# A hand-written schedule for every engine, half-batch broadcast tiles and later row sums in a three-point interpolation kernel

## The chip, the cores and the metric

The kernel runs on one core of a Trainium2 chip. The metric is the time of one execution in device microseconds. The engines are named as in the profile: PE multiplies matrices, PEld loads its weights, DVE works on vectors, ACT computes activations and copies, SP here only issues DMAs. The core has 16 DMA engines. A name with a q (SPq, ACTq) is an engine's sequencer issuing a DMA.

Only one core runs, so there is no other die to compare with. "Slow" here means only that a run was over 1.5% above the fastest run of the same kernel.

## The reference

For each of 16 batches, 4096 queries pick three of 1024 feature rows of 64 numbers and add them with normalized weights:

```python
batch, n_query, n_ref, dim = 16, 4096, 1024, 64
weights_norm = weights / (np.sum(weights, axis=2, keepdims=True) + 1e-8)
for b in range(batch):
    for i in range(n_query):
        for k in range(3):
            result[b, i] += weights_norm[b, i, k] * features[b, indices[b, i, k]]
```

## The kernel before

The gather is done as matrix products. A `prep` step on DVE turns indices into 16-bit codes and weights into two fp16 versions (for even and for odd rows), and writes both to DRAM. `load` broadcasts a batch's codes to all 128 partitions of SBUF, the on-chip memory (`bcc`), its even-row weights to partitions 0 to 63 and its odd-row weights to 64 to 127 (`bcw`), and loads and scales the features (`fst`, `f16`). Then, per group of 2048 queries, ACT makes `y` from the codes (`stage1`) and DVE makes four one-hot planes `s` (`stage2`). Per chunk of 512 queries PE multiplies features by `s` into `acc` (`main`), the result is weighted into `x` (on odd chunks through an ACT copy `xc`), and 12 small matmuls sum rows into `pr` (`back`), which ACT copies to `og` for the store.

```python
def load(b):
    bcc = sb.tile([P, K, Q], i16, bufs=2, name="bcc")
    nc.sync.dma_start(out=bcc[:, :, :], in_=code_d.ap()[b].unsqueeze(0).to_broadcast([P, K, Q]))
    bcw = sb.tile([P, K, Q], fp16, bufs=2, name="bcw")
    for h in range(2):
        nc.sync.dma_start(out=bcw[h * D:(h + 1) * D, :, :],
                          in_=wt_d.ap()[h, b].unsqueeze(0).to_broadcast([D, K, Q]))
    fst = sb.tile([P, J * P], fp32, bufs=2, name="fst")
    nc.scalar.dma_start(out=fst[:, :], in_=features[b].rearrange("(l x) d -> l (x d)", l=P))
    f16 = sb.tile([P, J, P], fp16, bufs=2, name="f16")
    nc.scalar.mul(out=f16.rearrange("p j m -> p (j m)"), in_=fst[:, :], mul=0.5)
    return bcc, bcw, f16
# ... cut: stage1, stage2, main, back ...
for i in range(NGT * NC):                  # 128 chunks
    g, c = divmod(i, NC)
    # ... cut: every 8 chunks prep of 4 batches and load(b + 1) ...
    if g + 1 < NGT:
        stage2(g + 1, c)
    x = main(i)
    if xs is not None:
        back(i - 1, xs)                    # row sums one chunk late
    xs = x
    if g + 2 < NGT and c > 0:
        stage1(g + 2, c - 1)
```

The program gives only this order; a scheduler decides where each instruction ends up on its engine.

Of the kernel before, what the change touches and what calls it, by code (L numbers as in the profile page):

```python
# [13 lines left out]
def kernel(  # L14
# [26 lines left out]
    GR = 2048  # L41
    NC = GR // CH
    NG = Q // GR
# [3 lines left out]
    Alu = mybir.AluOpType  # L47

# [6 lines left out]
    nc.sync.dma_start(out=i2[:, :], in_=i2_d.ap())  # L55
    bias_d = nc.inline_tensor((-8.0 * ((np.arange(P, dtype=np.float32) + 64) % 128 - 64))[:, None].copy(), name="lane")
    bias = sb.tile([P, 1], fp32, bufs=1, name="lane_sb")
    nc.sync.dma_start(out=bias[:, :], in_=bias_d.ap())
# [4 lines left out]
    def prep(b0):  # L63
        bs = slice(b0, b0 + PB)
        idx = sb.tile([P, PB, T, K], i64, bufs=1, name="idx")
        nc.sync.dma_start(out=idx[:, :, :, :],
                          in_=indices[bs].rearrange("b (p t) k -> p b t k", t=T))
        wt = sb.tile([P, PB, T, K], fp32, bufs=1, name="wt")
        nc.scalar.dma_start(out=wt[:, :, :, :],
                            in_=weights[bs].rearrange("b (p t) k -> p b t k", t=T))  # L70
        low = idx.bitcast(i32).rearrange("p b t (k w) -> p b k t w", k=K)[:, :, :, :, 0]
        idk = sb.tile([P, PB * K, T], i32, bufs=1, name="idk")
        nc.vector.tensor_copy(out=idk.rearrange("p (b k) t -> p b k t", b=PB), in_=low)  # L73
        lane = sb.tile([P, PB * K, T], i32, bufs=1, name="lane_i")
        nc.vector.tensor_scalar(out=lane[:, :, :], in0=idk[:, :, :], scalar1=6, scalar2=127 << 9,  # L75
                                op0=Alu.logical_shift_left, op1=Alu.bitwise_and)
        ex = sb.tile([P, PB * K, T], i32, bufs=1, name="ex")
        nc.vector.tensor_scalar(out=ex[:, :, :], in0=idk[:, :, :], scalar1=23, scalar2=3 << 24,
                                op0=Alu.logical_shift_left, op1=Alu.bitwise_and)
        ex2 = sb.tile([P, PB * K, T], i32, bufs=1, name="ex2")  # L80
        nc.vector.tensor_scalar(out=ex2[:, :, :], in0=ex[:, :, :], scalar1=134 << 23, scalar2=None,
                                op0=Alu.bitwise_xor)
        code = sb.tile([P, PB, K, T], u16, bufs=1, name="code")
        nc.vector.scalar_tensor_tensor(  # L84
            out=code.rearrange("p b k t -> p (b k t)"),
            in0=ex2.rearrange("p x t -> p (x t)").bitcast(fp32), scalar=0.5,
            in1=lane.rearrange("p x t -> p (x t)"), op0=Alu.mult, op1=Alu.add)
        hb = sb.tile([P, PB * K, T], i32, bufs=1, name="hb")
        nc.vector.tensor_scalar(out=hb[:, :, :], in0=idk[:, :, :], scalar1=1, scalar2=None,  # L89
                                op0=Alu.bitwise_and)  # L90
        ws = sb.tile([P, PB, T], fp32, bufs=1, name="ws")
        nc.vector.tensor_reduce(out=ws[:, :, :], in_=wt[:, :, :, :],  # L92
                                axis=mybir.AxisListType.X, op=Alu.add)
        nc.vector.tensor_scalar(out=ws[:, :, :], in0=ws[:, :, :], scalar1=1e-8, scalar2=None,
                                op0=Alu.add)
        wi = sb.tile([P, PB, T], fp32, bufs=1, name="wi")
        nc.vector.reciprocal(out=wi[:, :, :], in_=ws[:, :, :])  # L97
        wn = sb.tile([P, PB, K, T], fp16, bufs=1, name="wn")
# [32 lines left out]
    def stage1(g, k):  # L131
        b, gg = divmod(g, NG)
        if k == 0:
            ys[g] = sb.tile([P, K, GR], u8, bufs=2, name="y")
# [112 lines left out]
```

## Time and profile before

| | before |
|---|---|
| time, median (lowest to highest) | 523.24 us (522.9 to 523.54, 4 runs) |
| span of the profiled run | 521.9 us |
| first matmul | 63.0 us |
| DMA busy, all queues (85.5% of the span) | 446 us |
| ACT waiting for features | 2.3 us |

The page of the kernel before: span, PE's busy time, tenths busy in 40 slices of 13 us, and the main DMA queue (packets, MB, share of the 16 engines' span).

```profile
span 521.9 us, 7246 instructions
...
PE 402.1 (77%) x3072; PEld 203.2 (39%) x3072; DVE 303.9 (58%) x312; ACT 316.3 (61%) x242; POOL 0.2 (0%) x4
...
PE   0000188898988986898989797868989798989995
...
DMA  7999820798898879999999399999999899998421
...
q1 hardware_dynamic: 43296, 120.22, 81.9%
```

PE has nothing to do for 63 us and is then mostly 70 to 90% busy. The DMA engines, but for a gap in the start, are nearly always busy.

The windows view of the kernel before: busy time of each engine in each stretch, then the granted PE clock, the DMA share and GB/s. The first stretch loads `bcw`, the second `bcc`; the third is one cycle of a batch.

```profile
250.00:252.00 2.00, 2.00 (x22) 1.10 (x20) 0.00 (x0) 1.28 (x1) 0.00 (x0) 1.00 0.97 197
266.00:268.00 2.00, 2.00 (x21) 1.15 (x20) 1.29 (x2) 1.19 (x2) 0.00 (x0) 1.00 0.94 406
245.40:271.70 26.30, 24.49 (x193) 12.49 (x192) 16.61 (x16) 19.48 (x16) 0.00 (x0) 1.00 1.01 297
```

Both loads keep the engines busy, but `bcw` moves half as many bytes a second.

### The profile page before, as it was taken

The numbers are of one execution on the slowest core, as the hardware profiler recorded it, in microseconds if no ns is written. First come the engines' busy times: TensorE is split into PE (matmuls) and PEld (weight loads), VectorE is DVE, ScalarE is ACT, GpSimd is POOL, SyncE is SP. The second block draws the span as 40 slices with busy tenths as digits, with TensorE's granted clock in tenths as the row PEclk, the third lists the DMA queues.
The fourth block names the chain that finished last, engine by engine and source line by source line (L and its number), as shares of the span: only waits on it lengthen the run. The fifth ranks groups of instructions, "written<-read, shape, count | busy, mean of one in ns | idle before, by whom it ended". The sixth has DMA issues, their size and how long they took to land.

```text
span 521.9 us, 7246 instructions
## 1 busy us (share of the span) xinstructions
PE 402.1 (77%) x3072; PEld 203.2 (39%) x3072; DVE 303.9 (58%) x312; ACT 316.3 (61%) x242; POOL 0.2 (0%) x4
## 2 busy tenths in 40 slices
PE   0000188898988986898989797868989798989995
PEld 0000044444544443444544353434545354534443
DVE  5401375738584764656585855646585838484752
ACT  1006318667676838595868639385867768676733
POOL 0000000000000000000000000000000000000000
PEclk9999999998999999999999998989999999999998
DMA  7999820798898879999999399999999899998421
GB/s 187 339 195 315 167 51 30 299 218 329 202 343 213 172 284 224 377 215 374 215 377 215 112 315 211 370 212 374 212 372 212 325 230 332 235 331 203 124 80 42
DMA packets 47745, 125.67 MB, mean 241 GB/s; under 512 B 23136, under 2 KB 41568, under 8 KB 43616
## 3 DMA queue, kind: packets, MB, share of 16 engines
q1 hardware_dynamic: 43296, 120.22, 81.9%
q10 hardware_dynamic: 4416, 4.98, 3.2%
q8 instruction: 24, 0.39, 0.3%
q14 instruction: 9, 0.07, 0.1%
HBM read 107.23 MB, written 17.96 MB: 240 GB/s over the span
## 4 chain that ended last, share of the span: by engine, by line
PE 43%; ACT 19%; DMA 18%; issue 9%; DVE 9%; SPq 2%; DVEq 0%; ACTq 0%
PE acc L155 36%; ACT y L135 12%; DMA bcc<-code_d 8%; DMA wt<-in_weights_dram 8%; PE pr L177 7%; ACT xc L163 6%; DMA idx<-in_indices_dram 3%; DVE s L141 3%; DVE x L166 2%; DVE x L164 2%; SPq L111 1%; ACT og L184 1%; SPq L186 0%; SPq L120 0%; DVE idk L73 0%
## 5 line engine op out<-in xcount | busy, mean ns | idle before, releaser
L155 PE MATMUL acc<-s,f 128*128 128x512 fp8e4 x1536 | 367.3, 386 | 104.3 <-DVE s L141 70.5
L155 PEld LDWEIGHTS <-f 128*128 128x128 f16 x1536 | 143.7, 99 | 268.0 <-issue 114.9
L135 ACT ACTIVATE y<-bcc,lane_sb 128x2048 uint8<-128x2048 int16 x96 | 186.0, 1999 | 5.5 <-DMA bcc<-code_d 5.5
L141 DVE TENSOR_SCALAR s<-y 128x1536 int32<-128x1536 int32 x128 | 115.8, 955 | 64.2 <-ACT y L135 62.4
L163 ACT CAST xc<-acc 128x1536 f16<-128x1536 f32 x64 | 92.1, 1438 | 95.1 <-PE acc L155 95.1
L166 DVE TENSOR_TENSOR x<-acc,bcw 128x1536 f16<-128x1536 f32 x64 | 112.4, 1756 | 34.0 <-PE acc L155 33.5
L164 DVE TENSOR_TENSOR x<-xc,bcw 128x1536 f16<-128x1536 f16 x64 | 61.1, 955 | 69.7 <-ACT xc L163 69.7
L177 PEld LDWEIGHTS <-x 128*128 128x128 f16 x1536 | 70.0, 117 | 46.8 <-DVE x L164 18.6
L177 PE MATMUL pr<-i_sb,x 128*128 128x64 f16 x1536 | 72.8, 198 | 11.8 <-DVE x L164 10.0
L184 ACT COPY og<-pr 128x512 f32<-128x512 f32 x64 | 36.1, 588 | 60.7 <-PE pr L177 59.6
L92 DVE TENSOR_REDUCE ws<-wt 128x128 f32<-128x384 f32 x4 | 2.2, 550 | 41.8 <-DMA wt<-in_weights_dram 41.8
L135 ACT ACT_TABLE_LOAD x1 | 1.3, 1283 | 36.6 <-DVE wn L100 36.6
L125 ACT ACTIVATE f<-fst 128x512 f16<-128x512 f32 x16 | 10.1, 634 | 2.3 <-DMA fst<-in_features_dram 2.3
L73 DVE COPY idk<-idx 128x384 int32<-128x384 int32 x4 | 2.0, 504 | 3.4 <-DMA idx<-in_indices_dram 3.4
L97 DVE RECIPROCAL wi<-ws 128x128 f32<-128x128 f32 x4 | 3.8, 953 | 0.1
L100 DVE TENSOR_TENSOR wn<-wt,wi 128x128 f16<-128x128 f32 x12 | 3.3, 321 | 0.1
L125 ACT ACT_TABLE_LOAD x1 | 1.3, 1283 | 2.2 <-issue 2.2
L105 DVE TENSOR_TENSOR wh<-wn,hb 128x384 f16<-128x384 f16 x4 | 2.2, 556 | 0.0
L84 DVE SCALAR_TENSOR_TENSOR code<-ex,lane_i 128x384 uint16<-128x384 f32 x4 | 2.2, 554 | 0.0
L106 DVE TENSOR_TENSOR wh<-wn,wh 128x384 f16<-128x384 f16 x4 | 1.4, 359 | 0.1
L75 DVE TENSOR_SCALAR lane_i<-idk 128x384 int32<-128x384 int32 x4 | 1.4, 356 | 0.0
L89 DVE TENSOR_SCALAR hb<-idk 128x384 int32<-128x384 int32 x4 | 1.4, 358 | 0.0
(7 smaller groups left out, 4.2 us busy)
## 6 DMA issues: line engine op xcount, KB each, us to landing
bcc<-code_d SPq DMA_DIRECT2D x16, 3072.0 KB, 14.4
bcw<-wt_d SPq DMA_DIRECT2D x32, 1536.0 KB, 17.1
out_dram<-og SPq DMA_DIRECT2D x64, 256.0 KB, 7.4
fst<-in_features_dram ACTq DMA_DIRECT2D x16, 256.0 KB, 6.6
idx<-in_indices_dram SPq DMA_DIRECT2D x4, 384.0 KB, 5.0
wt<-in_weights_dram ACTq DMA_DIRECT2D x4, 192.0 KB, 10.2
wt_d<-wh SPq DMA_DIRECT2D x8, 96.0 KB, 7.0
code_d<-code SPq DMA_DIRECT2D x4, 96.0 KB, 7.3
```

What stands on the lines that cost most here:

```text
L97: nc.vector.reciprocal(out=wi[:, :, :], in_=ws[:, :, :])
L100: nc.vector.tensor_tensor(out=wn[:, :, k, :], in0=wt[:, :, :, k], in1=wi[:, :, :], op=Alu.mult)
L111: nc.sync.dma_start(out=wt_d.ap()[h, bs].rearrange("b k (p t) -> p b k t", t=T), in_=wh[:, h])
L125: nc.scalar.mul(out=f16.rearrange("p j m -> p (j m)"), in_=fst[:, :], mul=0.5)
L135: nc.scalar.activation(out=ys[g][:, k, :], in_=loaded[b][0][:, k, gg * GR:(gg + 1) * GR], func=Act.Abs_reciprocal_sqrt, bias=bias[:, :], s ...
L141: nc.vector.tensor_scalar(out=ss[g][:, j].rearrange("p k q -> p (k q)").bitcast(i32), in0=ys[g].rearrange("p k q -> p (k q)").bitcast(i32) ...
L155: nc.tensor.matmul(out=acc[:, k, :], lhsT=f16[:, j, :], rhs=s[:, j, k, c * CH:(c + 1) * CH], start=(j == 0), stop=(j == J - 1))
L163: nc.scalar.copy(out=xc[:, :, :], in_=acc[:, :, :])
L164: nc.vector.tensor_tensor(out=x[:, :, :], in0=xc[:, :, :], in1=w, op=Alu.mult)
L166: nc.vector.tensor_tensor(out=x[:, :, :], in0=acc[:, :, :], in1=w, op=Alu.mult)
L177: nc.tensor.matmul(out=pr[0][:, half, u, :], lhsT=x[:, k, :].rearrange("p (i u) -> p u i", u=U)[:, u, :], rhs=i2[:, :], start=(half == 0 a ...
L184: nc.scalar.copy(out=og[:, :, :, :], in_=pr[0][:, :, :, :])
```

## The change

The intent: no engine should idle because of the order a scheduler chose. Every instruction is kept in program order on its engine, and the program order is written out as a list of (time in chunks, step). The first batch is prepared alone and in small pieces, so that PE starts early. Broadcast tiles hold half a batch, with three buffers, and are asked for 12 chunks (codes) and 7 chunks (weights) ahead. All DMAs go through SP. The row sums of a chunk come two chunks late.

```diff
+    class InOrder:
+        def __getattr__(self, op):
+            def run(*a, **kw):
+                return tc.keep_in_program_order(getattr(self.engine, op)(*a, **kw))
+            return run
+    pe, ve, ac, sp = (InOrder(e) for e in (nc.tensor, nc.vector, nc.scalar, nc.sync))
 # ... cut ...
+    def load_codes(g):
+        b, q, n, _ = groups[g]
+        bcc[g] = sb.tile([P, K * GM], i16, bufs=3, name="bcc")[:, 0:K * n]
+        sp.dma_start(
+            out=bcc[g].rearrange("p (k q) -> p k q", k=K),
+            in_=code_d.ap()[b, :, q:q + n].unsqueeze(0).to_broadcast([P, K, n]))
 # ... cut: load_weights, the same with two halves of 64 partitions ...
+    def load_features(b):
         fst = sb.tile([P, J * P], fp32, bufs=2, name="fst")
-        nc.scalar.dma_start(out=fst[:, :], in_=features[b].rearrange("(l x) d -> l (x d)", l=P))
-        f16 = sb.tile([P, J, P], fp16, bufs=2, name="f16")
-        nc.scalar.mul(out=f16.rearrange("p j m -> p (j m)"), in_=fst[:, :], mul=0.5)
+        sp.dma_start(out=fst[:, :], in_=features[b].rearrange("(l x) d -> l (x d)", l=P))
+        f16s[b] = sb.tile([P, J, P], fp16, bufs=2, name="f16")
+        ac.mul(out=f16s[b].rearrange("p j m -> p (j m)"), in_=fst[:, :], mul=0.5)
 # ... cut ...
+    for g, (b, q, n, a) in enumerate(groups):      # a: first chunk of the group
+        m = n // CH
+        at(a - 12, 0, load_codes, g)
+        at(a - 7, 0, load_weights, g)
+        if q == 0:
+            at(a - 11.5 if b == 0 else a - 6, 0, load_features, b)
+        for c in range(m):
+            at(a - 2 * m + c if m == 4 else -8.5 + g / 10, 1, stage1, g, c)
+        for j in range(J):
+            at(a - m + (j * m // J | 1 if m == 4 else 0), 0, stage2, g, j)
 # ... cut ...
-        if xs is not None:
-            back(i - 1, xs)
+        if i >= 2:
+            back(i - 2, held[i - 2])
```

A half batch of codes is three runs of 4 KB per partition in DRAM, where a whole batch was one run of 24 KB.

More of the change, by code (lines that the diff above doesn't have):

```diff
@@ L40 @@
     CH = 512
-    GR = 2048
-    NC = GR // CH
-    NG = Q // GR
+    GM = 2048
     PB = 4
@@ L47, with __init__ @@
     Alu = mybir.AluOpType
+    class InOrder:
+        def __init__(self, engine):
+            self.engine = engine
+        def __getattr__(self, op):
[3 more added lines that the diff above has]
+    pe, ve, ac, sp = (InOrder(e) for e in (nc.tensor, nc.vector, nc.scalar, nc.sync))
     sb = ctx.enter_context(tc.tile_pool(name="sb", bufs=2))
@@ L54 @@
     i2 = sb.tile([P, D], fp16, bufs=1, name="i2_sb")
-    nc.sync.dma_start(out=i2[:, :], in_=i2_d.ap())
-    bias_d = nc.inline_tensor((-8.0 * ((np.arange(P, dtype=np.float32) + 64) % 128 - 64))[:, None].copy(), name="lane")
+    bias_d = nc.inline_tensor(
+        (-8.0 * ((np.arange(P, dtype=np.float32) + 64) % 128 - 64))[:, None].copy(), name="lane")
     bias = sb.tile([P, 1], fp32, bufs=1, name="lane_sb")
-    nc.sync.dma_start(out=bias[:, :], in_=bias_d.ap())
     code_d = nc.dram_tensor("code_d", [B, K, Q], i16, kind="Internal")
@@ L61 @@
     wt_d = nc.dram_tensor("wt_d", [2, B, K, Q], fp16, kind="Internal")
-    def prep(b0):
-        bs = slice(b0, b0 + PB)
-        idx = sb.tile([P, PB, T, K], i64, bufs=1, name="idx")
-        nc.sync.dma_start(out=idx[:, :, :, :],
-                          in_=indices[bs].rearrange("b (p t) k -> p b t k", t=T))
-        wt = sb.tile([P, PB, T, K], fp32, bufs=1, name="wt")
-        nc.scalar.dma_start(out=wt[:, :, :, :],
-                            in_=weights[bs].rearrange("b (p t) k -> p b t k", t=T))
-        low = idx.bitcast(i32).rearrange("p b t (k w) -> p b k t w", k=K)[:, :, :, :, 0]
-        idk = sb.tile([P, PB * K, T], i32, bufs=1, name="idk")
-        nc.vector.tensor_copy(out=idk.rearrange("p (b k) t -> p b k t", b=PB), in_=low)
-        lane = sb.tile([P, PB * K, T], i32, bufs=1, name="lane_i")
-        nc.vector.tensor_scalar(out=lane[:, :, :], in0=idk[:, :, :], scalar1=6, scalar2=127 << 9,
-                                op0=Alu.logical_shift_left, op1=Alu.bitwise_and)
-        ex = sb.tile([P, PB * K, T], i32, bufs=1, name="ex")
-        nc.vector.tensor_scalar(out=ex[:, :, :], in0=idk[:, :, :], scalar1=23, scalar2=3 << 24,
-                                op0=Alu.logical_shift_left, op1=Alu.bitwise_and)
-        ex2 = sb.tile([P, PB * K, T], i32, bufs=1, name="ex2")
-        nc.vector.tensor_scalar(out=ex2[:, :, :], in0=ex[:, :, :], scalar1=134 << 23, scalar2=None,
-                                op0=Alu.bitwise_xor)
-        code = sb.tile([P, PB, K, T], u16, bufs=1, name="code")
-        nc.vector.scalar_tensor_tensor(
-            out=code.rearrange("p b k t -> p (b k t)"),
-            in0=ex2.rearrange("p x t -> p (x t)").bitcast(fp32), scalar=0.5,
-            in1=lane.rearrange("p x t -> p (x t)"), op0=Alu.mult, op1=Alu.add)
-        hb = sb.tile([P, PB * K, T], i32, bufs=1, name="hb")
-        nc.vector.tensor_scalar(out=hb[:, :, :], in0=idk[:, :, :], scalar1=1, scalar2=None,
-                                op0=Alu.bitwise_and)
-        ws = sb.tile([P, PB, T], fp32, bufs=1, name="ws")
-        nc.vector.tensor_reduce(out=ws[:, :, :], in_=wt[:, :, :, :],
-                                axis=mybir.AxisListType.X, op=Alu.add)
-        nc.vector.tensor_scalar(out=ws[:, :, :], in0=ws[:, :, :], scalar1=1e-8, scalar2=None,
-                                op0=Alu.add)
-        wi = sb.tile([P, PB, T], fp32, bufs=1, name="wi")
-        nc.vector.reciprocal(out=wi[:, :, :], in_=ws[:, :, :])
-        wn = sb.tile([P, PB, K, T], fp16, bufs=1, name="wn")
-        for k in range(K):
-            nc.vector.tensor_tensor(out=wn[:, :, k, :], in0=wt[:, :, :, k], in1=wi[:, :, :],
-                                    op=Alu.mult)
-        wh = sb.tile([P, 2, PB, K, T], fp16, bufs=1, name="wh")
-        w1 = wh[:, 1].rearrange("p b k t -> p (b k) t")
-        wnf = wn.rearrange("p b k t -> p (b k) t")
-        nc.vector.tensor_tensor(out=w1, in0=wnf, in1=hb[:, :, :], op=Alu.mult)
-        nc.vector.tensor_tensor(out=wh[:, 0].rearrange("p b k t -> p (b k) t"), in0=wnf, in1=w1,
-                                op=Alu.subtract)
-        nc.sync.dma_start(out=code_d.ap()[bs].rearrange("b k (p t) -> p b k t", t=T),
-                          in_=code.bitcast(i16))
-        for h in range(2):
-            nc.sync.dma_start(out=wt_d.ap()[h, bs].rearrange("b k (p t) -> p b k t", t=T),
-                              in_=wh[:, h])
@@ L114, in load @@
-    def load(b):
-        bcc = sb.tile([P, K, Q], i16, bufs=2, name="bcc")
-        nc.sync.dma_start(out=bcc[:, :, :],
-                          in_=code_d.ap()[b].unsqueeze(0).to_broadcast([P, K, Q]))
-        bcw = sb.tile([P, K, Q], fp16, bufs=2, name="bcw")
-        for h in range(2):
-            nc.sync.dma_start(out=bcw[h * D:(h + 1) * D, :, :],
-                              in_=wt_d.ap()[h, b].unsqueeze(0).to_broadcast([D, K, Q]))
-        fst = sb.tile([P, J * P], fp32, bufs=2, name="fst")
-        nc.scalar.dma_start(out=fst[:, :], in_=features[b].rearrange("(l x) d -> l (x d)", l=P))
-        f16 = sb.tile([P, J, P], fp16, bufs=2, name="f16")
-        nc.scalar.mul(out=f16.rearrange("p j m -> p (j m)"), in_=fst[:, :], mul=0.5)
-        return bcc, bcw, f16
@@ L128, with prep, tl, loads @@
-    loaded = {}
-    ys, ss = {}, {}
-    def stage1(g, k):
-        b, gg = divmod(g, NG)
-        if k == 0:
-            ys[g] = sb.tile([P, K, GR], u8, bufs=2, name="y")
-        nc.scalar.activation(out=ys[g][:, k, :], in_=loaded[b][0][:, k, gg * GR:(gg + 1) * GR],
+    def prep(b0, n):
+        bs = slice(b0, b0 + n)
+        NK = n * K
+        def tl(dt, w, name):
+            return sb.tile([P, PB * w], dt, bufs=1, name=name)[:, 0:n * w]
+        idx = tl(i64, T * K, "idx")
+        wt = tl(fp32, T * K, "wt")
+        wt4 = wt.rearrange("p (b t k) -> p b t k", b=n, k=K)
+        idk = tl(i32, K * T, "idk")
+        lane = tl(i32, K * T, "lane_i")
+        ex = tl(i32, K * T, "ex")
+        code = tl(u16, K * T, "code")
+        hb = tl(i32, K * T, "hb")
+        ws = tl(fp32, T, "ws")
+        wi = tl(fp32, T, "wi")
+        wn = tl(fp16, K * T, "wn")
+        wh = [tl(fp16, K * T, "wh%d" % h) for h in range(2)]
+        v = ve
+        def loads():
+            sp.dma_start(out=idx.rearrange("p (b t k) -> p b t k", b=n, k=K),
+                              in_=indices[bs].rearrange("b (p t) k -> p b t k", t=T))
+            sp.dma_start(out=wt4, in_=weights[bs].rearrange("b (p t) k -> p b t k", t=T))
+        def weigh(k):
+            v.tensor_tensor(
+                out=wn.rearrange("p (b k t) -> p b k t", b=n, k=K)[:, :, k, :],
+                in0=wt4[:, :, :, k], in1=wi.rearrange("p (b t) -> p b t", b=n), op=Alu.mult)
+        def put(dst, src):
+            sp.dma_start(out=dst.rearrange("b k (p t) -> p (b k) t", t=T),
+                              in_=src.rearrange("p (x t) -> p x t", t=T))
+        return [
+            loads,
+            lambda: v.tensor_copy(
+                out=idk.rearrange("p (b k t) -> p b k t", b=n, k=K),
+                in_=idx.bitcast(i32).rearrange("p (b t k w) -> p b k t w", b=n, k=K, w=2)[:, :, :, :, 0]),
+            lambda: v.tensor_scalar(out=lane, in0=idk, scalar1=6, scalar2=127 << 9,
+                                    op0=Alu.logical_shift_left, op1=Alu.bitwise_and),
+            lambda: v.tensor_scalar(out=ex, in0=idk, scalar1=23, scalar2=3 << 24,
+                                    op0=Alu.logical_shift_left, op1=Alu.bitwise_and),
+            lambda: v.tensor_scalar(out=ex, in0=ex, scalar1=134 << 23, scalar2=None,
+                                    op0=Alu.bitwise_xor),
+            lambda: v.scalar_tensor_tensor(out=code, in0=ex.bitcast(fp32), scalar=0.5, in1=lane,
+                                           op0=Alu.mult, op1=Alu.add),
+            lambda: put(code_d.ap()[bs], code.bitcast(i16)),
+            lambda: v.tensor_reduce(out=ws, in_=wt.rearrange("p (x k) -> p x k", k=K),
+                                    axis=mybir.AxisListType.X, op=Alu.add),
+            lambda: v.tensor_scalar(out=ws, in0=ws, scalar1=1e-8, scalar2=None, op0=Alu.add),
+            lambda: v.reciprocal(out=wi, in_=ws),
+            lambda: weigh(0),
+            lambda: weigh(1),
+            lambda: weigh(2),
+            lambda: v.tensor_scalar(out=hb, in0=idk, scalar1=1, scalar2=None, op0=Alu.bitwise_and),
+            lambda: v.tensor_tensor(out=wh[1], in0=wn, in1=hb, op=Alu.mult),
+            lambda: v.tensor_tensor(out=wh[0], in0=wn, in1=wh[1], op=Alu.subtract),
+            lambda: put(wt_d.ap()[0, bs], wh[0]),
+            lambda: put(wt_d.ap()[1, bs], wh[1]),
+        ]
@@ new lines @@
+    groups = []
+    for b in range(B):
+        q = 0
+        for n in ([512, 512, 1024, 2048] if b == 0 else [2048, 2048]):
+            groups.append((b, q, n, (b * Q + q) // CH))
+            q += n
+    owner = {}
+    for g, (b, q, n, a) in enumerate(groups):
+        for c in range(n // CH):
+            owner[a + c] = (g, c)
+    bcc, bcw, f16s, ys, ss = {}, {}, {}, {}, {}
+    def load_codes(g):
[4 more added lines that the diff above has]
+            in_=code_d.ap()[b, :, q:q + n].unsqueeze(0).to_broadcast([P, K, n]))
@@ new lines, in load_weights @@
+    def load_weights(g):
+        b, q, n, _ = groups[g]
+        bcw[g] = sb.tile([P, K * GM], fp16, bufs=3, name="bcw")[:, 0:K * n].rearrange(
+            "p (k q) -> p k q", k=K)
+        for h in range(2):
+            sp.dma_start(
+                out=bcw[g][h * D:(h + 1) * D],
+                in_=wt_d.ap()[h, b, :, q:q + n].unsqueeze(0).to_broadcast([D, K, n]))
+    def load_features(b):
+        fst = sb.tile([P, J * P], fp32, bufs=2, name="fst")
+        sp.dma_start(out=fst[:, :], in_=features[b].rearrange("(l x) d -> l (x d)", l=P))
+        f16s[b] = sb.tile([P, J, P], fp16, bufs=2, name="f16")
+        ac.mul(out=f16s[b].rearrange("p j m -> p (j m)"), in_=fst[:, :], mul=0.5)
@@ L136, in stage1 @@
+    def stage1(g, c):
+        if c == 0:
+            ys[g] = sb.tile([P, K * GM], u8, bufs=2, name="y")
+        w = K * CH
+        ac.activation(out=ys[g][:, c * w:(c + 1) * w], in_=bcc[g][:, c * w:(c + 1) * w],
                              func=Act.Abs_reciprocal_sqrt, bias=bias[:, :], scale=1.0 / 64)
     def stage2(g, j):
+        n = K * groups[g][2]
         if j == 0:
-            ss[g] = sb.tile([P, J, K, GR], u8, bufs=2, name="s")
-        nc.vector.tensor_scalar(
-            out=ss[g][:, j].rearrange("p k q -> p (k q)").bitcast(i32),
-            in0=ys[g].rearrange("p k q -> p (k q)").bitcast(i32),
+            ss[g] = sb.tile([P, J, K * GM], u8, bufs=2, name="s")
+        ve.tensor_scalar(
+            out=ss[g][:, j, 0:n].bitcast(i32), in0=ys[g][:, 0:n].bitcast(i32),
@@ L147, in main @@
     def main(i):
-        g, c = divmod(i, NC)
-        b, gg = divmod(g, NG)
-        _, bcw, f16 = loaded[b]
-        s = ss[g].bitcast(fp8)
+        g, c = owner[i]
+        b, _, n, _ = groups[g]
+        s = ss[g][:, :, 0:K * n].bitcast(fp8).rearrange("p j (k q) -> p j k q", k=K)
         acc = ps.tile([P, K, CH], fp32, bufs=2, name="acc")
@@ L154, in main, with weight @@
             for j in range(J):
-                nc.tensor.matmul(out=acc[:, k, :], lhsT=f16[:, j, :],
+                pe.matmul(out=acc[:, k, :], lhsT=f16s[b][:, j, :],
                                  rhs=s[:, j, k, c * CH:(c + 1) * CH],
                                  start=(j == 0), stop=(j == J - 1))
-        x = sb.tile([P, K, CH], fp16, bufs=3, name="x")
-        q0 = gg * GR + c * CH
-        w = bcw[:, :, q0:q0 + CH]
+        return acc
+    def weight(i, acc):
+        g, c = owner[i]
+        x = sb.tile([P, K, CH], fp16, bufs=4, name="x")
+        w = bcw[g][:, :, c * CH:(c + 1) * CH]
         if i % 2:
             xc = sb.tile([P, K, CH], fp16, bufs=2, name="xc")
-            nc.scalar.copy(out=xc[:, :, :], in_=acc[:, :, :])
-            nc.vector.tensor_tensor(out=x[:, :, :], in0=xc[:, :, :], in1=w, op=Alu.mult)
+            ac.copy(out=xc[:, :, :], in_=acc[:, :, :])
+            ve.tensor_tensor(out=x[:, :, :], in0=xc[:, :, :], in1=w, op=Alu.mult)
         else:
-            nc.vector.tensor_tensor(out=x[:, :, :], in0=acc[:, :, :], in1=w, op=Alu.mult)
+            ve.tensor_tensor(out=x[:, :, :], in0=acc[:, :, :], in1=w, op=Alu.mult)
         return x
@@ L176, in back @@
             for k in range(K):
-                nc.tensor.matmul(
+                pe.matmul(
                     out=pr[0][:, half, u, :],
@@ L183, in back @@
             og = sb.tile([P, 2, U, D], fp32, bufs=3, name="og")
-            nc.scalar.copy(out=og[:, :, :, :], in_=pr[0][:, :, :, :])
+            ac.copy(out=og[:, :, :, :], in_=pr[0][:, :, :, :])
             b, c = divmod(i, Q // CH)
-            nc.sync.dma_start(
+            sp.dma_start(
                 out=out[b, (c - 1) * CH:(c + 1) * CH].rearrange("(c i u) d -> i c (u d)", c=2, u=U),
                 in_=og.rearrange("p c u d -> p c (u d)"))
-    NGT = B * NG
-    prep(0)
-    loaded[0] = load(0)
@@ L193 @@
-    for k in range(K):
-        stage1(0, k)
-    for j in range(J):
-        stage2(0, j)
-    for k in range(K):
-        stage1(1, k)
-    xs = None
-    for i in range(NGT * NC):
-        g, c = divmod(i, NC)
-        if i % (NG * NC) == 0:
-            b = i // (NG * NC)
-            if b % PB == 0 and b + PB < B:
-                prep(b + PB)
-            if b + 1 < B:
-                loaded[b + 1] = load(b + 1)
-        if g + 1 < NGT:
-            stage2(g + 1, c)
-        x = main(i)
-        if xs is not None:
-            back(i - 1, xs)
-        xs = x
-        if g + 2 < NGT and c > 0:
-            stage1(g + 2, c - 1)
@@ L216, with at @@
-    back(NGT * NC - 1, xs)
+    todo = []
+    def at(time, engine, f, *args):
+        todo.append((time, len(todo), engine, f, args))
+    for g, (b, q, n, a) in enumerate(groups):
+        m = n // CH
[7 more added lines that the diff above has]
+            at(a - m + (j * m // J | 1 if m == 4 else 0), 0, stage2, g, j)
@@ new lines @@
+    NCH = B * Q // CH
+    for b0 in range(PB, B, PB):
+        for s, step in enumerate(prep(b0, PB)):
+            at((b0 - 4) * (Q // CH) + (s and s + 3), 0, step)
+    first, second = prep(0, 1), prep(1, PB - 1)
+    at(-20, 0, first[0])
+    at(-20, 0, second[0])
+    for step in first[1:]:
+        at(-19, 0, step)
+    for s, step in enumerate(second):
+        if s:
+            at(-5.5 if s in (6, 16, 17) else -8.9, 0, step)
+    todo.sort(key=lambda t: t[:2])
+    warm = sb.tile([P, 1], fp32, bufs=1, name="warm")
@@ new lines, with run @@
+    sp.dma_start(out=bias[:, :], in_=bias_d.ap())
+    warm2 = sb.tile([P, 1], fp32, bufs=1, name="warm2")
+    ve.memset(warm[:, :], 1.0)
+    ac.activation(out=warm2[:, :], in_=warm[:, :], func=Act.Abs_reciprocal_sqrt, bias=bias[:, :],
+                  scale=0.5)
+    sp.dma_start(out=i2[:, :], in_=i2_d.ap())
+    def run(engine, time):
+        while todo and todo[0][0] < time:
+            if todo[0][2] != engine:
+                break
+            _, _, _, f, args = todo.pop(0)
+            f(*args)
@@ new lines @@
+    while todo[0][0] < 0:
+        run(0, 0)
+        run(1, 0)
+    held = []
+    for i in range(NCH):
+        now = [t for t in todo if t[0] < i + 1]
+        del todo[:len(now)]
+        for _, _, late, f, args in now:
+            if not late:
+                f(*args)
+        acc = main(i)
+        held.append(weight(i, acc))
+        if i >= 2:
+            back(i - 2, held[i - 2])
+        for _, _, late, f, args in now:
+            if late:
+                f(*args)
+    back(NCH - 2, held[NCH - 2])
@@ L220 @@
+    back(NCH - 1, held[NCH - 1])
 _INS = ['features', 'indices', 'weights']
```

## The prediction

It was written before the changed kernel had run. Two passages that gave a mechanism for the half rate of `bcw` are cut where marked, since no trace or run of this case shows that mechanism.

> **What bounds it now.** The loop is not held by arithmetic. In an undisturbed stretch a 512-query chunk costs PE 2.98 us (timeline: 2.59 us of products into acc, 0.39 us to pr), so 128 chunks need 382 us. Per chunk DVE needs about 2.3 us (s 0.91, half of 1.70 + 0.955), ACT about 2.6. The span is 521.9 us: 63 us pass before the first matmul (waits: PE waits 63.0 us on s), and the rest runs at 3.6 us a chunk.
>
> I think the limit of that rest is the DMA engines. The queue table gives 85% of 16 engines over the span, 446 us. In the windows view, one batch cycle (245.4 to 271.7 us) has DMA share 1.01 in 26.3 us; PE needs 23.9. The reason is the weight broadcast: while bcw loads, DMA is 0.97 busy at 197 GB/s; while bcc loads, 0.94 busy at 406. bcw goes as two DMAs of 64 partitions. [...] (24 KB packets take about 1,930 ns for bcw, 912 ns for bcc). Per batch: bcw 14.9 us, bcc 7.3, out 3.15, features 0.7: about 26.1 us. Other idle time comes from loads asked for late (chain of waits: 13 and 27 us on bcc) and from the start (wt loads behind whole-batch broadcasts, landing at 40 and 60 us).
>
> **What the change does.** Arithmetic and bytes stay. The start prepares batch 0 alone and cuts it into 512, 512, 1024 and 2048 queries; first matmul at about 13 us instead of 63. Tiles are half batches, three buffers, asked for 12 and 7 chunks ahead, so the DMA queue should always hold work. y is 128x1536 per instruction (estimate 1.5 us, from 1.99 for 2048). Row sums two chunks late give x nearly 6 us instead of 3; no PE stall is left there. The 64-partition form of the bcw loads stays. Packets shrink from 24 KB to 4 KB; estimated from 2 KB packets at 84 ns, a bcc packet takes about 160 ns, 5% more than its bytes need (6 us in all).
>
> **Sum.** DMA becomes the one limit. 16 batches of 26.1 to 26.5 us are 418 to 424 us; index, weight and 64-byte writes another 22: 440 to 447. Broadcasts start near 8 us with about 2.5 us of work done; the last outputs (6 us) follow the last load. So the last bcw lands near 440 to 447 us; the last chunks then take about 13 us (two DVE products, two PE chunks, copies, store). With 1 to 2% of gaps: 463 us. PE alone would give some 410 to 415 us, which I do not expect.
>
> Predicted 464 us, range 448 to 485. Faster by over 2%: 0.96; within: 0.03; slower: 0.01.
>
> **What would show it.** First matmul between 11 and 17 us; DMA digits 9 from the second slice nearly to the end; DVE x waiting for bcw; a two-group cycle of about 26.5 us; windows with bcw at about 200 GB/s. Row-summing matmuls hardly ever wait for x, except after a bcw wait.
>
> **What would make it wrong.** If the 4 KB packets of the two bcw halves overlap[...], the time falls towards 415 us. If 4 KB packets cost clearly more than 160 ns, or waits in the single DMA queue (stores wait for compute ahead of loads) leave gaps, it goes above 480. If the fixed order makes DVE wait for idx in front of x, a few us are lost per preparation.

## More of the kernel before

The view of the tile `fst` in the kernel before: the loads and the copies that read them (durations, then the start of the first and of the last).

```profile
L123 ACTq DMA_DIRECT2D fst<-in_features_dram x16: 334/334/523, 1.2 to 411.3; - x16
L125 ACT ACTIVATE f<-fst x16: 618/633/647, 4.9 to 464.8; 128x512 f16<-128x512 f32 x16
...
  DMA fst<-in_features_dram: 2.3, 2
...
DMA to landing us min/median/max: 2.7/6.6/18.0
```

The last load was issued at 411.3 us and its copy ran at 464.8 us: the scheduler had put some 50 us between them, although the program text has them in adjacent lines.

## The result, and the profile after

The changed kernel took 644.61 us (643.55 to 649.85, 4 runs) against 523.24 us before. The ratio is 1.2337, with a 95% interval of 1.2278 to 1.2396. Here and below a ratio is the mean time of one kernel's fast runs over that of the other's of the same rounds, so it is not quite the ratio of the medians quoted.

| | before | after |
|---|---|---|
| time, median | 523.24 us | 644.61 us |
| span of the profiled run | 521.9 us | 647.9 us |
| first matmul | 63.0 us | 19.4 us |
| DMA busy, all queues | 446 us | 510 us |
| ACT waiting for features | 2.3 us | 234.8 us |

The page of the changed kernel, the same lines (a slice is now 16 us):

```profile
span 647.9 us, 7370 instructions
...
PE 419.7 (65%) x3072; PEld 211.8 (33%) x3072; DVE 306.5 (47%) x335; ACT 321.6 (50%) x274; POOL 0.2 (0%) x4
...
PE   0435492957859294793929649294875939387596
...
DMA  5899495896959599695969959699795959669521
...
q1 hardware_dynamic: 70672, 125.20, 78.4%
```

PE starts 44 us earlier, but it falls to 2 or 3 tenths over and over, and DMA falls with it, to 4 to 6 tenths. Had DMA been the one limit, as predicted, its row would be 9 throughout. Something else stops both, about once a batch.

The view of the tile `fst` in the changed kernel:

```profile
L55 SPq DMA_DIRECT2D fst<-in_features_dram x16: 459/468/2944, 9.0 to 588.0; - x16
L55 ACT ACTIVATE f<-fst x16: 629/629/629, 16.8 to 603.3; 128x512 f16<-128x512 f32 x16
...
  DMA fst<-in_features_dram: 234.8, 16
...
DMA to landing us min/median/max: 6.4/14.6/15.8
```

Every one of the 16 copies `f` now waits, 14.7 us each. The last load is issued 15 us before its copy runs, instead of 53. From the waits of this run (who waited for whom: us in total, times, longest), that wait and the one it leads to:

```profile
ACT f L55 <- DMA fst<-in_features_dram: 234.8, 16, 19.1
...
PE acc L55 <- ACT xc L55: 196.7, 16, 15.8
```

One such stop in the timeline of the changed kernel (start, duration, engine, what it does, in brackets the idle time before it and who ended it):

```profile
242.81 1.59 ACT L55 ACTIVATE y<-bcc,lane_sb 128x1536 uint8<-128x1536 int16 x1
242.95 10.80 SPq L55 DMA_DIRECT2D out_dram<-og  x1
...
249.71 0.56 PE L55 MATMUL pr<-i_sb,x 128*128 128x64 f16 x12
...
253.81 2.94 SPq L55 DMA_DIRECT2D fst<-in_features_dram  x1
260.50 0.63 ACT L55 ACTIVATE f<-fst 128x512 f16<-128x512 f32 x1 [16.10 <-DMA fst<-in_features_dram]
261.03 1.56 ACT L55 ACTIVATE y<-bcc,lane_sb 128x1536 uint8<-128x1536 int16 x1
262.50 1.42 ACT L55 CAST xc<-acc 128x1536 f16<-128x1536 f32 x1
263.82 0.59 ACT L55 COPY og<-pr 128x512 f32<-128x512 f32 x1
263.95 0.96 DVE L55 TENSOR_TENSOR x<-xc,bcw 128x1536 f16<-128x1536 f16 x1 [16.39 <-ACT xc L55]
263.97 4.43 PE L55 MATMUL acc<-s,f 128*128 128x512 fp8e4 x10 [13.70 <-ACT xc L55]
```

ACT has reached `f` at 244 us. Its load has not even been issued: SP stands for 10.8 us in the issue of a store in front of it (the median issue of a store takes 0.38 us in this run; what holds the long ones is not shown). The load lands at 260.5 us. Until then ACT may not do the copy `xc` that stands behind `f`, so `acc` is not freed, and PE, done at 250 us, waits 13.7 us. DVE waits 16.4 us. Three of the 16 loads came late in this way, behind a store's issue of 7.6 to 10.8 us, and then landed in 6.4 to 8.0 us. After the first batch the other 12 were issued without such a hold but took 13.9 to 15.8 us to land.

The windows view of the same stop:

```profile
252.00:254.00 2.00, 0.00 (x0) 0.00 (x0) 0.00 (x0) 0.00 (x0) 0.00 (x0) 1.00 1.08 202
...
260.00:262.00 2.00, 0.00 (x0) 0.00 (x0) 0.00 (x0) 1.50 (x2) 0.00 (x0) 0.50 0.00 0
...
264.00:266.00 2.00, 2.00 (x5) 0.66 (x5) 2.00 (x3) 2.00 (x3) 0.00 (x0) 0.50 0.33 109
```

While all engines stand still, DMA works off its backlog at 202 GB/s (a `bcw` rate); then it runs dry too (0.00), because the next loads stand in SP's order behind stores of results that ACT has not copied to `og` yet (ACT's copy starts at 263.82 us, SP issues the store at 264.43 and the next `bcc` at 264.86). So the stop costs DMA time as well. The granted PE clock fell as well: PE's last work before the stop ended at 250.3 us, the clock was 1.00 up to 255 us, 0.61 from 255 to 256, 0.50 from 256 to 268, 0.56 from 268 to 269, and then 1.00 again. In the chain of waits the first 12 products after the stop take 5.16 us, those of the chunks shortly before and after it 2.59.

### The profile page after: what moved, and what is told of

Same layout as the page of the kernel before. It is cut to its first block, busy times and chain, and to the rows that moved or that the text cites. A ratio compares the mean times of both kernels' runs of the same rounds, so it can differ in the third digit from the quotient of the medians.

```text
span 647.9 us, 7370 instructions
## 1 busy us (share of the span) xinstructions
PE 419.7 (65%) x3072; PEld 211.8 (33%) x3072; DVE 306.5 (47%) x335; ACT 321.6 (50%) x274; POOL 0.2 (0%) x4
## 4 chain that ended last, share of the span: by engine, by line
PE 41%; DMA 36%; ACT 10%; SPq 7%; issue 4%; DVE 2%; ACTq 0%
PE acc L55 37%; DMA fst<-in_features_dram 31%; SPq L55 7%; ACT y L55 4%; DMA bcc<-code_d 4%; PE pr L55 4%; ACT xc L55 4%; ACT og L55 1%; DVE x L55 1%; DVE s L55 1%; DMA code_d<-code 0%; DMA idx<-in_indices_dram 0%; ACTq L55 0%; ACT f L55 0%; DVE wn L55 0%
## 5 line engine op out<-in xcount | busy, mean ns | idle before, releaser
L55 PE MATMUL acc<-s,f 128*128 128x512 fp8e4 x1536 | 386.6, 406 | 222.8 <-ACT xc L55 196.7
L55 PEld LDWEIGHTS <-f 128*128 128x128 f16 x1536 | 151.0, 103 | 401.7 <-issue 244.7
L55 ACT ACTIVATE y<-bcc,lane_sb 128x1536 uint8<-128x1536 int16 x128 | 196.7, 1576 | 17.0 <-DMA bcc<-code_d 17.0
L55 ACT ACTIVATE f<-fst 128x512 f16<-128x512 f32 x16 | 10.1, 629 | 234.8 <-DMA fst<-in_features_dram 234.8
L55 DVE TENSOR_SCALAR s<-y 128x1536 int32<-128x1536 int32 (+2 forms) x136 | 117.0, 904 | 15.4 <-ACT y L55 15.4
L55 DVE RECIPROCAL wi<-ws 128x128 f32<-128x128 f32 (+2 forms) x5 | 3.9, 789 | 0.1
L55 DVE TENSOR_TENSOR wn<-wt,wi 128x128 f16<-128x128 f32 (+2 forms) x15 | 3.9, 284 | 0.1
L55 DVE COPY idk<-idx 128x384 int32<-128x384 int32 (+2 forms) x5 | 2.5, 493 | 3.0 <-DMA idx<-in_indices_dram 3.0
L55 DVE SCALAR_TENSOR_TENSOR code<-ex,lane_i 128x384 uint16<-128x384 f32 (+2 forms) x5 | 2.4, 474 | 0.2 <-DMA code_d<-code 0.2
L55 DVE TENSOR_TENSOR wh<-wn,hb 128x384 f16<-128x384 f16 (+2 forms) x5 | 2.4, 474 | 0.1
L55 DVE TENSOR_REDUCE ws<-wt 128x128 f32<-128x384 f32 (+2 forms) x5 | 2.3, 466 | 0.0
## 6 DMA issues: line engine op xcount, KB each, us to landing
fst<-in_features_dram SPq DMA_DIRECT2D x16, 256.0 KB, 14.6
bcw<-wt_d SPq DMA_DIRECT2D x4, 192.0 KB, 10.8
```

The costliest lines, as they stand in the source:

```text
L55: return tc.keep_in_program_order(getattr(self.engine, op)(*a, **kw))
```

## The experiments

The theory after this reading was: the copy `f` is pinned right behind its own load, the load is the last entry of a deep DMA queue (14.6 us from issue to landing), and everything on ACT waits for it (A). The rivals: the DMA engines themselves became slower (510 us busy against 446), or the hand-written order as such is bad. All twelve kernels gave correct results. The kernel before, run beside them, had medians of 524.25 to 524.83 us.

### 1. The feature load eight chunks earlier, the copy where it was

```diff
-            at(a - 11.5 if b == 0 else a - 6, 0, load_features, b)
+            at(a - 11.5 if b == 0 else a - 14, 0, load_features, b)
+            at(a - 11.5 if b == 0 else a - 6, 0, scale_features, b)
```

> Edit: the fixed order stays, but each batch's feature load is asked for 8 chunks earlier (14 chunks ahead of its batch instead of 6), while the scaling copy f on ACT keeps its place (6 ahead). Theory A (the copy f stands in ACT's fixed order right behind its own load, which is the last entry of a DMA queue some 15 us deep; ACT waits 235 us for it over the run, the copies xc wait behind it, acc is not freed and PE stops): ACT's wait for fst falls from 235 us to under 20, no PE stall of 15 us is left, and the time falls to about 465 us (450 to 490), where the DMA engines are the limit as I had predicted. Rival B (the DMA engines themselves are now slower: 4 KB packets and one queue, 510 us of busy time in the changed kernel's profile against 446 before): the time stays at 520 us or above, with DMA digits of 9 nearly everywhere. Rival C (the hand-written order as such, many in-order waits): above 560 us.

Measured: 536.67 us (530.28 to 538.94), ratio to before 1.0158 (1.0093 to 1.0223). Groups of instructions in this run, with the idle time before them, and its DMA queue:

```profile
q1 hardware_dynamic: 70672, 125.20, 92.9%
...
L55 ACT ACTIVATE y<-bcc,lane_sb 128x1536 uint8<-128x1536 int16 x128 | 200.0, 1578 | 156.8 <-DMA bcc<-code_d 156.7
...
L55 ACT ACTIVATE f<-fst 128x512 f16<-128x512 f32 x16 | 10.0, 624 | 12.9 <-DMA fst<-in_features_dram 12.9
```

The wait for features is gone except for the first batch (12.9 us), and with it about 110 us. So A holds for the largest part. But the expected 450 to 490 us were not reached: DMA is now busy 93.2% of 537.0 us, that is 500 us, as rival B said, and ACT waits for codes.

### 2. The feature load on ACT's own queue, in its late place

```diff
-        sp.dma_start(out=fst[:, :], in_=features[b].rearrange("(l x) d -> l (x d)", l=P))
+        ac.dma_start(out=fst[:, :], in_=features[b].rearrange("(l x) d -> l (x d)", l=P))
```

> Edit: the feature load is issued on ACT's own DMA queue, as the kernel before did, at the same place of the fixed order, with the copy f right behind it. Theory A: the load no longer stands behind the other queue's backlog; issue to landing falls from 14.6 us to about 4 to 7 us and ACT's wait for it from 235 us to 60 to 110; time 490 to 550 us, between the changed kernel and the early load. Rival B (DMA bandwidth): the wait is as long, since the engines are full anyway; time above 600 us.

Measured: 533.29 us (520.9 to 537.8); only one of the four runs counts as fast, so there is no interval. ACT's wait for features was 56.5 us in 16 times, at most 5.0; the load landed after 7.9 us (median) instead of 14.6; both lie just outside what was expected. With a DMA share of 0.95 (245.4 to 271.7 us), the load on the other queue landed in about half the time that it took on SP's; how the engines share their time between queues was not shown. So most of the wait was not the load itself but what stood before it on SP. This run also takes the load out of SP's order, where it could stand behind a store's long issue; the two effects are not separated.

### 3. The same program without the pinned order

```diff
-                return tc.keep_in_program_order(getattr(self.engine, op)(*a, **kw))
+                return getattr(self.engine, op)(*a, **kw)
```

> Edit: the same program, tiles and buffers, but no instruction is kept in program order, so the scheduler orders each engine as it did in the kernel before (in its order f stands several copies behind its load). Theory A: most of the stalls go; time 470 to 540 us, ACT's wait for fst under 100 us. Rival D (the half-batch tiles and small packets are what costs, not the order): stays above 600 us.

Measured: 535.31 us (529.56 to 542.66), ratio 1.01 (1.0062 to 1.0138). The scheduler put other copies between load and `f`, and the wait for features was 1.6 us. Note that runs 1 and 3 take nearly the same time with entirely different orders (fast runs: 532.7 and 529.6 us on average), with DMA busy 93% of both: while DMA was the limit here, the order did not matter. That the pinned order is bad in itself falls.

### 4. The kernel before, with weights on even and odd partitions

```diff
-    i2_np = np.concatenate([np.eye(D), np.eye(D)], 0).astype(np.float16)
+    i2_np = np.repeat(np.eye(D), 2, axis=0).astype(np.float16)
-            nc.sync.dma_start(out=bcw[h * D:(h + 1) * D, :, :],
+            nc.sync.dma_start(out=bcw[h:P:2, :, :],
-        nc.scalar.mul(out=f16.rearrange("p j m -> p (j m)"), in_=fst[:, :], mul=0.5)
+        nc.scalar.mul(out=f16.rearrange("p j (d h) -> p j h d", h=2),
+                      in_=fst.rearrange("p (j h d) -> p j h d", j=J, h=2), mul=0.5)
```

> Edit to the kernel BEFORE: the two 64-partition weight broadcasts go to the even and to the odd partitions instead of the lower and the upper half (columns of the scaled features and the summing matrix are permuted to match; the result is the same). If the half rate of bcw comes from 64 neighbouring partitions[...], and if that is what bounds the loop of the kernel before, its 24 KB packets fall from about 1,930 ns towards 912 to 1,100 ns, DMA busy time from 446 us to about 330 to 360, and the time to 470 to 500 us. Rival 1[...]: packets stay near 1,900 ns and the time within 1%. Rival 2 (rate doubles, but the loop was not DMA-bound): packets fall, time stays within 2% of before.

Measured: 506.24 us, ratio 0.9661 (0.9625 to 0.9696). The 24 KB packets fell from 1,395 to 1,013 ns on average. Windows of this run; the first lies in a `bcw` load (issued at 234.9 us, before the next `bcc` at 248.2), the second is a cycle of the same length as before:

```profile
238.00:240.00 2.00, 2.00 (x12) 0.95 (x11) 0.91 (x1) 0.14 (x1) 0.00 (x0) 1.00 0.94 393
...
245.40:271.70 26.30, 24.49 (x194) 12.48 (x192) 17.63 (x16) 19.63 (x16) 0.00 (x0) 1.00 0.77 289
```

DMA busy time fell to 68.0% of 507.0 us, 345 us, and a batch cycle has DMA share 0.77 instead of 1.01. So the half rate came with the contiguous halves of the partitions: 197 GB/s there, 393 in steps of two. What in the hardware makes the difference was not shown. (Below, "balanced" means this even and odd layout, "half-rate" the other; the expectation of run 7 calls the layout "the ports".) But taking 101 us of DMA time away gained 18 us, and the time missed the expected 470 to 500 us. In the traces, 10 of the 16 batches take the same time in both kernels to 0.02 us, from first product to first product (most of them 26.8 or 27.4 us). Of the 14.9 us between the two profiled runs, 10.4 are an earlier first matmul (63.0 to 52.6 us), and the rest is about what one batch gained in which `bcc` had come late (36.1 to 30.4 us). So in the undisturbed cycles DMA did not set the pace of the kernel before, although its share there was 1.01. That the order set it is not isolated by this run; run 7, with a written-out order and other tiles, takes 23.9 us a batch.

### 5. The early load with 12 KB packets

The DRAM copies are laid out by half batch, so that a half-batch broadcast reads one run of 12 KB per partition.

```diff
-    code_d = nc.dram_tensor("code_d", [B, K, Q], i16, kind="Internal")
-    wt_d = nc.dram_tensor("wt_d", [2, B, K, Q], fp16, kind="Internal")
+    code_d = nc.dram_tensor("code_d", [2, B, K, GM], i16, kind="Internal")
+    wt_d = nc.dram_tensor("wt_d", [2, 2, B, K, GM], fp16, kind="Internal")
```

(The writes and reads of these tensors are changed to match.)

> Edit on top of the early feature load (535 us): the DRAM copies of codes and weights are laid out by half batch, so that each half-batch broadcast reads one contiguous 12 KB run per partition instead of three of 4 KB. The early load left DMA busy time at 500 us against 446 in the kernel before. Theory P (packet size: 4 KB packets of the broadcasts cost far more than the 6 us I predicted, 390 us busy against 357 with 24 KB packets[...]): busy time falls to about 450 us, and the time to 470 to 490 us. Rival Q (the deep single queue mixes half-rate bcw packets with the others, whatever their size): busy time stays near 500 us and the time within 2% of 535.

Measured: 504.42 us (496.94 to 509.08), ratio 0.9513 (0.9454 to 0.9572). DMA busy fell to 92.2% of 507.3 us, 468 us. So theory P holds for 33 of the 54 us of DMA time by which run 1 exceeded the kernel before, and the fast runs agree (532.7 to 499.4 us on average). Packet size and layout in DRAM change together here and are not separated. The time is above the expected range; as in run 1 (shown at run 12), some 30 us of work still follow the last loads.

### 6. The early load with even and odd partitions

> Edit on top of the early feature load (535 us): the two bcw halves go to even and odd partitions, as in the run on the kernel before, where 24 KB packets fell from 1,395 to 1,013 ns on average. If what is left after the early load is DMA time of half-rate bcw loads: mean 4 KB packet from 262 to 170 to 190 ns, DMA busy from 500 to under 380 us, PE becomes the limit (128 chunks of 2.98 us after a start of about 30 us): 415 to 440 us. Rival (issue cost per packet and in-order waits[...]): 490 us or more.

The edit is that of run 4 on run 1. Measured: 435.91 us, ratio 0.8307 (0.829 to 0.8323). The chain of work that ended last, as shares of this run's span:

```profile
PE 86%; DMA 6%; SPq 3%; ACT 3%; DVE 1%; issue 1%; ACTq 0%
PE acc L55 75%; PE pr L55 11%; SPq L55 3%; DMA bcc<-code_d 3%; DMA fst<-in_features_dram 2%; ACT xc L55 2%; ACT y L55 1%; DMA idx<-in_indices_dram 1%; DMA code_d<-code 0%; ACT f L55 0%; ACT og L55 0%; DVE x L55 0%; DVE wn L55 0%; DVE wi L55 0%; DVE ws L55 0%
```

In run 1 the same chain is 60% DMA and 15% PE. DMA busy is down from 500 to 388 us (89.5% of 434.0), a 4 KB packet takes 194 ns on average instead of 262 (both slightly more than I expected), and PE is the limit.

### 7. Both together

> Both edits together on top of the early feature load: even and odd partitions, and 12 KB packets. If [...] packets matter less, 410 to 430 us and within 2% of the run with the ports alone; if packet size matters as much, clearly faster than that run.

Measured: 432.49 us, ratio 0.8241 (0.8221 to 0.8261). DMA busy falls further, to 359 us (83.2% of 431.2), but PE is the limit already, so 30 us of DMA time are worth 3.

### 8. Row sums one chunk late instead of two, on run 6

```diff
-        if i >= 2:
-            back(i - 2, held[i - 2])
+        if i >= 1:
+            back(i - 1, held[i - 1])
```

> Edit on top of early load plus even/odd partitions: the row-summing matmuls one chunk late, as in the kernel before, instead of two. x of an odd chunk is ready about 2.45 us after its products (copy 1.43, product 0.96), and PE comes to the row sums after 2.6 us, so little margin: I expect 0 to 3% slower than with two chunks, with PE or its weight load waiting for x some 10 us in total. If the two chunks are what keeps PE fed, more than 5% slower.

Measured: 438.05 us, ratio to before 0.8343 (0.8328 to 0.8358) against 0.8307: 0.4% more. This part of the change is worth little.

### 9. Even and odd partitions on the changed kernel, the feature load left late

> Edit on the changed kernel itself: only the even/odd partitions for bcw; the feature load keeps its late place right in front of its copy f. If ACT's 235 us of waiting for fst were a consequence of the DMA backlog[...], the wait shrinks to 50 to 110 us (3 to 7 us a batch) and most of it fits into ACT's spare time: 440 to 475 us, close to the 436 us with the early load as well. If the place of the load is a fault of its own, independent of the backlog, the wait stays above 150 us and the time above 500 us.

Measured: 565.27 us, ratio 1.0776 (1.0725 to 1.0826). My expectation failed: the time is above 500 us, and the wait, 147.6 us, is far above 110 and just below the 150 named for the other case. From the waits of this run (who waited for whom: us in total, times, longest):

```profile
ACT f L55 <- DMA fst<-in_features_dram: 147.6, 16, 12.9
...
PE acc L55 <- ACT xc L55: 112.3, 16, 12.4
```

With 413 us of DMA busy time (73.2% of 564.2) in place of 510, the load still lands 9.0 us after its issue (median), and ACT has no such reserve. So the late place of the load is a fault that does not need the half-rate weights: it costs about 130 us here (565 against 436). It is not shown to be independent of the backlog: the wait fell from 235 to 148 us with the weights' rate, and with little in front of it the same load lands in 2.7 us (the shortest in the kernel before).

### 10. The start, on run 7

```diff
-            at(a - 11.5 if b == 0 else a - 14, 0, load_features, b)
+            at(-19.9 if b == 0 else a - 14, 0, load_features, b)
-            at(a - 2 * m + c if m == 4 else -8.5 + g / 10, 1, stage1, g, c)
+            at(a - 2 * m + c + (g == 4) if m == 4 else -8.5 + g / 10, 1, stage1, g, c)
```

> Edit on the fastest version so far (early load, even/odd partitions, 12 KB packets: 432.5 us): at the start the first features are asked for right behind the first indices and weights instead of behind the first code broadcast, and the y instructions of batch 1 come one chunk later in ACT's order, so that the copy xc of chunk 1 no longer waits for the codes of batch 1 (PE waited 9.8 us on it). PE is at its 2.98 us a chunk in the rest, so only the start can give: first matmul from 20.8 to about 16 us, and 420 to 428 us in all. If the start is bound by the DMA queue anyway, within 1% of 432.

Measured: 426.63 us (426.56 to 429.19), ratio 0.8141 (0.811 to 0.8171). The gain of 6 us is within the expected range; the first matmul came at 18.4 us, not 16. The two edits are not separated. This is the fastest version, 19% below the kernel before and about 34% below the changed kernel.

### 11. Run 7 without the pinned order

> Edit on the same 432.5 us version: nothing is kept in program order, the scheduler orders each engine. If the hand-written order is worth something once DMA is out of the way: 445 to 490 us (the kernel before with even/odd partitions, in the scheduler's order, took 506 with its longer start). If the order is worth nothing: within 2% of 432.

The edit is that of run 3. Measured: 535.31 us, ratio 1.02 (1.0174 to 1.0226): slower than I expected from the loss of the order, and 103 us slower than run 7. ACT in this run's timeline:

```profile
251.73 0.79 ACT L55 ACTIVATE f<-fst 128x512 f16<-128x512 f32 x1
252.37 0.57 ACT L55 COPY og<-pr 128x512 f32<-128x512 f32 x1
258.57 1.44 ACT L55 CAST xc<-acc 128x1536 f16<-128x1536 f32 x1 [5.63 <-PE acc L55]
259.90 5.98 ACT L55 ACTIVATE y<-bcc,lane_sb 128x1536 uint8<-128x1536 int16 x4
265.78 1.42 ACT L55 CAST xc<-acc 128x1536 f16<-128x1536 f32 x1
267.10 1.08 ACT L55 COPY og<-pr 128x512 f32<-128x512 f32 x2
274.41 1.44 ACT L55 CAST xc<-acc 128x1536 f16<-128x1536 f32 x1 [6.24 <-PE acc L55]
```

The scheduler puts four `y` (6 us) in a row between two copies, and then ACT idles about 6 us. Over the run DVE waits 143 us for `y`, ACT waits 193 us for products, and PE waits 71 us for `xc`. The pinned order spreads them two by two. A batch takes 32.0 us here and 23.9 in run 7; in run 4 the scheduler's order of the other program took 26.8 to 27.4. So the 103 us are measured against a poor order of this program, not against any order of a scheduler.

### 12. Codes asked for 16 chunks ahead, on run 1

```diff
-        at(a - 12, 0, load_codes, g)
+        at(a - 16 if g >= 6 else a - 12, 0, load_codes, g)
```

> Edit on the early feature load (535 us): the code broadcasts are asked for 16 chunks ahead instead of 12 (from the third batch on). In that run ACT waited 157 us for codes and nobody for weights, and after the DMA engines had finished their loads, at about 503 us, 33 us of work were left, because codes are needed 8 chunks before their products. If the tight deadline of the codes costs that tail, the last loads are followed by a shorter tail and waits move from codes to weights: 510 to 525 us. If DMA time alone decides, the time stays within 1%.

The reason for this run is the end of run 1, in windows:

```profile
492.00:498.00 6.00, 5.92 (x48) 3.12 (x47) 3.08 (x3) 0.01 (x1) 0.00 (x0) 1.00 1.03 236
...
504.00:510.00 6.00, 6.00 (x47) 3.07 (x46) 3.88 (x5) 4.67 (x4) 0.00 (x0) 0.90 0.24 82
...
522.00:528.00 6.00, 6.00 (x50) 3.15 (x48) 2.75 (x3) 1.93 (x2) 0.00 (x0) 1.00 0.13 44
```

DMA is done with its loads at about 503 us, and 33 us of compute follow. Measured: 552.59 us (542.08 to 555.39, one fast run, no interval). The expectation failed. The waits did move, from codes (157 to 17 us) to weights (DVE's waits for `bcw`: 1 to 91 us):

```profile
ACT og L55 <- DMA out_dram<-og: 138.5, 25, 9.5
DVE x L55 <- DMA bcw<-wt_d: 90.6, 22, 8.1
```

The tail shortened only to 28 us, and ACT, in its fixed order, now waited 139 us for stores to finish. The loads ended later, at about 524 us. It looks as if loads asked for earlier in the one full queue delayed the stores behind them, but this was not tested further. Since three of its four runs are slow, I take from this run only that asking earlier did not help; whether the tail could be cut otherwise is open.

## Why the prediction was wrong

**The step that failed first** is "DMA becomes the one limit". The prediction let tiles "asked for 12 and 7 chunks ahead" keep the queue full and allowed 1 to 2% of gaps. It counted the features as 0.7 us of DMA a batch, and did not ask where the copy `f` stands in ACT's order. The change pins `f` directly behind its own load. What the runs showed instead of one limit: ACT waits 234.8 us for features, and through `xc` PE waits 196.7 us. The prediction did list among its risks "waits in the single DMA queue (stores wait for compute ahead of loads)", and at the stop shown the queue ran dry in this way (0.00 at 260 us); but it named no load that compute would wait for, and gave "slower" 0.01. A full queue, which I counted as a good thing, goes with that late load: 14.6 us from issue to landing (median), against 7.9 on ACT's queue (run 2) and 9.0 with balanced weights (run 9). Run 1 removes this alone and gets about 110 us back (644.6 to 532.7, the mean of its two fast runs). Run 9 shows that it costs 130 us even where DMA is busy only 73% of the span.

**The DMA term was mis-sized.** The prediction had 440 to 447 us for DMA, of which 6 us for packets of 4 KB. Run 1 measured 500. Laying out the data for 12 KB packets took 33 us of this back (run 5, 468 us). The bcc packet alone was estimated right: the most frequent 4 KB packets in the changed kernel take 150 to 160 ns. But the 4 KB packets of both broadcasts average 262 ns in run 1, where a sixth of the 24 KB packets of before is 233. What makes up the remaining 22 us is not settled. The 1 KB packets, nearly all of them stores, also took longer (49 to 55 ns), and the packets of fast and half-rate loads follow each other closely in the queue (in run 1 a `bcc` was issued at 262.48 us and a `bcw` at 263.03); I did not separate these. With balanced loads 14 us of such a difference remain (run 7, 359 us, against run 4, 345), so half-rate loads are not all of it.

**The tail was mis-sized.** I expected 13 us of work behind the last load, assuming that the last load is a `bcw`. In run 1 it was the codes that everything waited for, and these are needed eight chunks ahead of their products: 33 us.

Taken together: 464 predicted, about 110 for the feature wait, about 50 for DMA, 20 for the tail make 644. That they add up so well is partly luck, since the terms are not independent.

**What was right.** The half rate of `bcw`. Run 4 shows that it belongs to the contiguous halves: a load of 64 partitions in steps of two, over both halves, lifts a `bcw` window from 197 to 393 GB/s, and runs 6 and 7 show the same in DMA busy time (500 to 388 us, and 468 in run 5 to 359). The mechanism behind it was not shown. The first matmul did move early (63.0 to 19.4 us), though less than the 11 to 17 us I had said. With two-chunk row sums PE hardly waits for `x` (1.7 us for the matmuls and 9.0 us for their weight loads in the changed kernel), but that is worth 0.4% (run 8). PE alone comes near the 410 to 415 us that I gave it: run 10, whose chain is 86% PE, is at 426.6 us.

**What was mostly wrong about the kernel before.** "I think the limit of that rest is the DMA engines": run 4 took 101 us of DMA time away for a gain of 18 us, most of it in the start, and its undisturbed batches kept their length. A DMA share of 1.01 showed that the engines were busy, not that the loop waited for them.

**What was right about the order.** In the changed program with 12 KB packets and balanced loads, the written-out order is worth 103 us against the scheduler's (run 11 against run 7). While DMA was the limit it was worth nothing (run 3 against run 1). So the idea of the change was sound; the changed program's own DMA time (500 us in run 1) hid it, and one misplaced load turned it into a loss.

## What to carry to other kernels

When you pin an engine's order, go through every instruction that consumes a DMA and ask when its load is issued and what stands before it in the queue. Here the distance had to cover 14.6 us from issue to landing (the median in the changed kernel), not the load's 2.7 us at its shortest, and one late operand stopped everything behind it on ACT (16.1 us idle at the stop shown). A rarely used small load is the easiest one to overlook: it was 10 us of ACT work and 235 us of waiting. In this program the order showed its worth only when DMA was no longer full (run 7 against 11, run 1 against 3): free the DMA engines first (here by which partitions a load writes), then order the work. And a busy resource is not yet the limit: in the kernel before it took an experiment (run 4) to tell.
